# One level of Strassen's scheme in the up projection of a gated MLP, with the down projection cut into four K parts

## The chip, the core and the metric

The kernel runs on one core of a Trainium2 chip. The metric is device time in microseconds for the whole program, from inputs in DRAM to the output in DRAM. The core's engines are named as the profile names them: PE multiplies matrices (PEld is its weight load), DVE, ACT and POOL work element by element, and SP issues transfers. All matrix products accumulate in PSUM; everything else lies in SBUF.

## The reference, cut to what matters

One decoder layer over 528 positions (16 meta tokens and 512 inputs) and 1024 channels. The first half of it (a chunked linear attention branch and a pooling branch, merged by gates) is left out here; the change reaches it only through its buffers. What matters is the second half:

```python
D_FF = 2816
h = h + (gate_a * y_a + gate_b * y_b) @ w_o[l]
hn = rmsnorm(h, norm2_g[l])
up = causal_dwconv(hn @ w_up[l], conv_w[l], conv_b[l])   # three taps
a, bv = jnp.split(up, 2, axis=-1)
h = h + (jax.nn.silu(a) * bv) @ w_down[l]
return rmsnorm(h, final_norm_g)[:, N_META:]
```

`w_up` is 1024 x 5632 and `w_down` is 2816 x 1024, all in float32.

## The kernel before

Activations lie with channels on the 128 partitions and positions along the row, so `h2` is eight tiles of 128 x 528. Each float32 product is made of three products of a shorter format (`F32R`): a tile is split into a high part (an ACT copy that rounds) and a low part (a DVE subtraction of the rounded copy), and hi x hi, hi x lo and lo x hi are accumulated. That is `products` (L112 to L122), with `split` (L217) for activations and `prep_chunk` (L93) for weights.

Weights come in 142 chunks of up to 128 x 1024 in the order of a table (`ORDER`, L46): SP loads a chunk (L91), ACT makes its high part (L102), DVE its low part (L103). Three buffers for the raw chunk and three for the parts let this run ahead of PE by two to three chunks (`chunk`, L105).

The up projection (L582) runs over 22 pairs of 128 output channels, side 0 for `a` and side 1 for `bv`. Each side is one `project`: 8 K tiles x 3 products x 2 halves of the positions (258 and 256 columns), 48 matmuls. DVE multiplies the result by the row's norm factor (L591); ACT and DVE apply the three taps (L594 to L596); ACT applies silu (L598); DVE multiplies the sides (L600), and ACT and DVE split the result into `gh` and `gl` (L601, by L218 and L219). The norm factor itself (`rstd2`) is ready only some microseconds after the first side's matmuls.

The down projection (L618) comes after all 22 pairs: 8 output tiles, each with 66 matmuls over the 22 K tiles, the last one as two halves of 256 positions (L631), behind each of which stands the final norm and the output for that half. A list scheduler of the compiler orders instructions of each engine as their inputs are expected; the engines then run their own lists in order.

SBUF is held by `bigp` (nine buffers of 8 x 528 values per partition) and small pools for weights and work.

Of the kernel before, what the change touches and what calls it, by code (L numbers as in the profile page):

```python
# [15 lines left out]
P = 128  # L16
# [16 lines left out]
UCOLS = (((12, 270), (270, L)), ((10, 270), (270, L)), ((6, 268), (268, L)), FULL)  # L33
SUPERS = [(0, 16)] + [(16 + 128 * i, 128) for i in range(4)]
# [13 lines left out]
for _name, _n in (  # L48
    ("k", 4), ("q", 4), ("v", 8), ("r", 8), ("u", 8), ("ga", 8), ("a", 8),
    ("gb", 8), ("grp", 2), ("b", 8), ("o", 8), ("up", 44), ("down", 24),  # L50
):
    ORDER[_name] = _at
    _at += _n
# [8 lines left out]
def hybrid_block(ctx: ExitStack, tc: tile.TileContext, xt, g1d, wts, wglr, wgk, vecs, out):  # L62
# [10 lines left out]
    def big(name, dt=F32, shape=(KT, L)):  # L73
        return bigp.tile([P, *shape], dt, tag="big", name=name)
# [9 lines left out]
    def load_chunk(j, cuts=None):  # L84
        if j >= NCHUNK or (j in raws and cuts is None):
            return
        nk = 6 if j >= ORDER["down"] and (j - ORDER["down"]) % 3 == 2 else KT
        if j not in raws:
            raws[j] = (wrawp.tile([P, KT, P], F32, tag="wraw", name=f"wraw{j}"), nk)
        for a, b in cuts or ((0, nk),):  # L90
            sp.dma_start(raws[j][0][:, a:b], wts[j, :, a:b])  # L91

    def prep_chunk(j, cuts=None):  # L93
# [3 lines left out]
        t, nk = raws[j]  # L97
# [3 lines left out]
        a, b = cuts or (0, nk)  # L101
# [22 lines left out]
    def project(name, j, xh, xl, cols, hook=None, ahead=PREP_AHEAD):  # L124
        hi, lo = chunk(j, ahead)
        acc = ps(name)
        products(acc, [(hi[:, k], lo[:, k], xh[:, k], xl[:, k]) for k in range(KT)], cols, hook=hook)
# [32 lines left out]
    sp.dma_start(x0[:, 0, 0:264], xt[0, :, 0:264])  # L160
    act.dma_start(g1, g1d)
    load_chunk(0, ((0, 2),))
    sp.dma_start(x0[:, 0, 264:], xt[0, :, 264:])
    load_chunk(1, ((0, 2),))
    sp.dma_start(x0[:, 1], xt[1])
    load_chunk(0, ((2, KT),))
    sp.dma_start(x0[:, 2], xt[2])
    load_chunk(1, ((2, KT),))
    for k in range(3, KT):
        sp.dma_start(x0[:, k], xt[k])  # L170
# [11 lines left out]
    for k in range(KT):  # L182
        for a, b in FULL if k == 0 else ((0, L),):
            act.activation(xh[:, k, a:b], x0[:, k, a:b], AF.Copy, scale=g1[:, k : k + 1])
            dve.scalar_tensor_tensor(xl[:, k, a:b], x0[:, k, a:b], g1[:, k : k + 1], f32(xh[:, k, a:b]), ALU.mult, ALU.subtract)
# [3 lines left out]
        if k >= 2:  # L189
            act.activation(sq1[:, k - 2], x0[:, k - 2], AF.Square)  # L190
# [531 lines left out]
```

## Time and profile before

| what | value |
|---|---|
| three runs | 861.96, 862.66, 862.73 us; median 862.66 |
| the profiled execution | span 860.6 us from its first to its last instruction; its time beside that isn't given, so what lies around it is taken as 862.66 - 860.6 = 2.1 us |
| PE busy | 847.6 us, 98% of the span, granted clock 1.00 between the ends |
| DVE, ACT, POOL busy | 485.0, 345.1, 62.3 us |
| up projection | from 475.9 to 728 us |
| down projection | from 728 to 849.6 us, with 11.0 us behind it |
| moved | 81.13 MB, mean 94 GB/s |

How to read it: a busy share is of the whole span or of a named stretch. A matmul's printed duration (some 282 ns for 258 columns) is longer than the step from one to the next, since matmuls overlap; steps are read from the chain of waits. On DVE, too, the next instruction may start some 0.08 us before the printed end of the one ahead.

### The profile page before, as it was taken

To read this page: it belongs to the slowest core of one execution; us is meant where nothing else is said; L and a number is where in the kernel's file an instruction comes from. 1 tells how busy PE (TensorE), PEld (TensorE's weight loads), DVE (VectorE), ACT (ScalarE), POOL (GpSimd) and SP (SyncE) were. 2 spreads that over 40 slices of the span, in tenths; PEclk is the share of its full clock that TensorE was granted. 3 is DMA by queue.
4 is the path that set the end of the run, shared out by engine and by line. 5 is a ranking of instruction groups with operands and counts; after the bars stand their busy time and mean duration, and the time that the engine had idled before them with its cause. 6 is when DMAs were issued, how large, how long until landed. Compare 5 with 4: busy or idle time off the path is not lost.

```text
span 860.6 us, 15278 instructions
## 1 busy us (share of the span) xinstructions
PE 847.6 (98%) x6627; PEld 824.5 (96%) x6627; DVE 485.0 (56%) x716; ACT 345.1 (40%) x479; POOL 62.3 (7%) x48
## 2 busy tenths in 40 slices
PE   8999999999999999999999999999999999999995
PEld 7999999999999999999999999999999999888884
DVE  6676445389647433355554677667776777332224
ACT  6378243256335212353234544444444444232231
POOL 4000000001740000000012100000000000001011
PEclk9999999999999999999999999999999999999998
DMA  7423311122332333225332333233323332332312
GB/s 241 123 74 99 87 61 50 50 75 74 99 98 75 98 98 99 84 89 196 98 88 85 99 98 85 89 98 99 90 83 98 98 95 79 95 101 85 97 39 98
DMA packets 25939, 81.13 MB, mean 94 GB/s; under 512 B 2864, under 2 KB 5680, under 8 KB 25872
## 3 DMA queue, kind: packets, MB, share of 16 engines
q1 hardware_dynamic: 24384, 78.84, 30.4%
q10 hardware_dynamic: 1488, 1.32, 0.5%
q8 instruction: 52, 0.85, 0.4%
q14 instruction: 15, 0.12, 0.0%
HBM read 78.05 MB, written 2.10 MB: 93 GB/s over the span
## 4 chain that ended last, share of the span: by engine, by line
PE 96%; DVE 1%; ACT 1%; DMA 1%; issue 0%; SPq 0%; DVEq 0%
PE pup L119 29%; PE pv L119 5%; PE pu L119 5%; PE pr L119 5%; PE pga L119 5%; PE po L119 5%; PE pb L119 5%; PE pgb L119 5%; PE pa L119 5%; PE pd L615 5%; PE pd L614 5%; PE pd L616 5%; PE pq L119 3%; PE pk L119 1%; PE pgrp L119 1%; PE po L415 1%
## 5 line engine op out<-in xcount | busy, mean ns | idle before, releaser
L102 ACT ACTIVATE whi<-wraw 128x1024 fp32r<-128x1024 f32 (+2 forms) x146 | 149.2, 1024 | 330.2 <-PE pd L615 71.0
L103 DVE TENSOR_TENSOR wlo<-wraw,whi 128x1024 fp32r<-128x1024 f32 (+2 forms) x146 | 175.9, 1206 | 78.8 <-ACT whi L102 68.8
L119 PE MATMUL pup<-h2l,whi 128*128 128x258 f32 x704 | 141.6, 282 | 0.0
L119 PE MATMUL pup<-h2h,whi 128*128 128x258 f32 x704 | 140.9, 282 | 0.0
L119 PE MATMUL pup<-h2h,wlo 128*128 128x258 f32 x704 | 140.8, 281 | 0.0
L119 PEld LDWEIGHTS pup<-h2h,wlo 128*128 128x128 f32 x704 | 108.8, 188 | 0.0
L119 PEld LDWEIGHTS pup<-h2h,whi 128*128 128x128 f32 x704 | 107.9, 188 | 0.0
L119 PEld LDWEIGHTS pup<-h2l,whi 128*128 128x128 f32 x704 | 107.8, 188 | 0.0
L614 PE MATMUL pd<-gh,whi 128*128 128x512 f32 (+1 forms) x198 | 72.7, 367 | 0.0
L615 PE MATMUL pd<-gl,whi 128*128 128x512 f32 (+1 forms) x198 | 72.4, 365 | 0.0
L616 PE MATMUL pd<-gh,wlo 128*128 128x512 f32 (+1 forms) x198 | 72.3, 365 | 0.0
L591 DVE TENSOR_TENSOR up<-pup,rstd 128x258 f32<-128x258 f32 x88 | 33.5, 421 | 45.9 <-PE pup L119 44.5
L614 PEld LDWEIGHTS pd<-gh,whi 128*128 128x128 f32 x198 | 37.3, 189 | 6.1
L616 PEld LDWEIGHTS pd<-gh,wlo 128*128 128x128 f32 x198 | 37.3, 189 | 6.0
L615 PEld LDWEIGHTS pd<-gl,whi 128*128 128x128 f32 x198 | 37.3, 189 | 6.0
L594 ACT ACTIVATE cv<-up,vec 128x512 f32<-128x512 f32 x44 | 35.9, 816 | 3.8 <-DVE up L591 3.2
L218 ACT ACTIVATE gh<-cv 128x512 fp32r<-128x512 f32 x22 | 13.9, 633 | 55.1 <-DVE cv L600 55.1
L596 DVE SCALAR_TENSOR_TENSOR cv<-up,vec,cv 128x512 f32<-128x512 f32 x44 | 33.1, 752 | 1.5
L595 DVE SCALAR_TENSOR_TENSOR cv<-up,vec,cv 128x512 f32<-128x512 f32 x44 | 32.9, 747 | 1.3 <-ACT cv L594 1.3
L627 POOL TENSOR_TENSOR sq<-sq,n_sq 128x512 f32<-128x512 f32 x6 | 7.8, 1296 | 348.0 <-ACT n_sq L626 348.0
L598 ACT ACTIVATE cv<-cv 128x512 f32<-128x512 f32 x22 | 13.9, 633 | 41.1 <-DVE cv L596 41.1
L574 POOL TENSOR_TENSOR n_sq<-n_sq,n_sq 128x514 f32<-128x514 f32 x7 | 12.4, 1778 | 220.5 <-ACT n_sq L570 220.5
(241 smaller groups left out, 1804.5 us busy)
## 6 DMA issues: line engine op xcount, KB each, us to landing
wraw<-in_wts_dram SPq DMA_DIRECT2D x132, 512.0 KB, 3.6
wraw<-in_wts_dram SPq DMA_DIRECT2D x10, 384.0 KB, 3.1
h<-in_xt_dram SPq DMA_DIRECT2D x1, 2056.0 KB, 8.8
x<-in_xt_dram SPq DMA_DIRECT2D x7, 264.0 KB, 5.9
out_dram<-h ACTq DMA_DIRECT2D x2, 384.0 KB, 2.8
out_dram<-h ACTq DMA_DIRECT2D x2, 256.0 KB, 2.3
out_dram<-h SPq DMA_DIRECT2D x2, 256.0 KB, 2.5
x<-in_xt_dram SPq DMA_DIRECT2D x2, 132.0 KB, 2.4
```

The lines of the kernel that those rows point to most:

```text
L102: act.activation(hi[:, a:b], t[:, a:b], AF.Copy)
L103: dve.tensor_tensor(lo[:, a:b], t[:, a:b], f32(hi[:, a:b]), ALU.subtract)
L119: pe.matmul(acc[:, s, : b - a], w, x[:, a:b], start=(i == 0 and w is wh and x is xh), stop=(i == n - 1 and last),)
L218: act.activation(hi, src, AF.Copy)
L591: dve.tensor_tensor(z[:, c], src, rstd2[:, c], ALU.mult)
L594: act.activation(cv, z[:, META:], AF.Identity, scale=v1("cw2", m), bias=v1("cb", m))
L595: dve.scalar_tensor_tensor(cv, z[:, META - 1 : L - 1], v1("cw1", m), cv, ALU.mult, ALU.add)
L596: dve.scalar_tensor_tensor(cv, z[:, META - 2 : L - 2], v1("cw0", m), cv, ALU.mult, ALU.add)
L598: last = act.activation(cv, cv, AF.Silu)
L614: pe.matmul(acc, hi[:, k], gh[part][:, k, a:b], start=first, stop=False)
L615: pe.matmul(acc, hi[:, k], gl[part][:, k, a:b], start=False, stop=False)
L616: pe.matmul(acc, lo[:, k], gh[part][:, k, a:b], start=False, stop=last)
```

## The change

The up projection's weights are seen as 2 x 2 blocks (two K groups of four tiles each: the even and the odd ones; two sides), and the normalised input as 2 x 2 blocks (two K groups, two halves of the positions, both of 258 columns now; they start at position 12, with zeros in front). One level of Strassen's scheme needs 7 block products for the 8. Each block product is 4 K tiles x 3 = 12 matmuls (`seven`), so a pair takes 84 matmuls where it took 96. The first three pairs (`PLAIN`) still take 96.

The scheme needs sums. On the input side they are made once, after the norm factor is known (`cross`): three blocks as they are (`direct`) and four sums (`crossed`), each split into high and low parts. On the weight side they are made for each pair (`make`): three blocks as they are (`gh`, `gl`) and four sums, in two tiles `sa` and `sb`. On the output side two of the seven products are added by PE in PSUM and the rest by ACT copies and four DVE operations per pair; the norm factor is in the input now and isn't applied again.

The low parts of the three plain weight blocks, and of all down weights, are made another way (`low_by_dma`): POOL writes the negated high part to `gl`, and a transfer issued by POOL adds the float32 weights from DRAM to it. So these weights are read from DRAM twice. `gh` and `gl` have two buffers each.

The down projection is cut into four K parts (6, 6, 6 and 4 tiles). The first three are put between the up pairs, two jobs of two output tiles each behind pairs 8, 9, 14, 15, 19 and 21, and add into `h2`; the last one comes at the end, again with the last tile in two halves, of 12 matmuls now.

The buffers of the first half are made of pairs of tiles in three pools; those that the second half doesn't need are closed before it, and six new pools lie in their place.

```diff
+H0 = 12
+HALF = ((H0, 270), (270, L))
+HN = 258
+PLAIN = 3
+LAG = 2
+PARTS = ((0, 6), (6, 6), (12, 6), (18, 4))
...
-    bigp = ctx.enter_context(tc.tile_pool(name="bigp", bufs=9))
-    wrawp = ctx.enter_context(tc.tile_pool(name="wrawp", bufs=3))
-    whlp = ctx.enter_context(tc.tile_pool(name="whlp", bufs=3))
-    work = ctx.enter_context(tc.tile_pool(name="work", bufs=5))
+    lastp = ctx.enter_context(tc.tile_pool(name="lastp", bufs=12))
+    first = ctx.enter_context(ExitStack())
+    firstp = first.enter_context(tc.tile_pool(name="firstp", bufs=16))
+    midp = first.enter_context(tc.tile_pool(name="midp", bufs=8))
+    wrawp = first.enter_context(tc.tile_pool(name="wrawp", bufs=3))
+    whlp = first.enter_context(tc.tile_pool(name="whlp", bufs=3))
+    work = first.enter_context(tc.tile_pool(name="work", bufs=5))
...
-    s2 = None
+    n2t = wk("n2t")
+    first.close()
+    def phase(name, bufs):
+        return ctx.enter_context(tc.tile_pool(name=name, bufs=bufs, reuse_waits="tile"))
+    rawp, gp, sump, ssp, t3p, unitp = (
+        phase(*a) for a in (("rawp", 2), ("gp", 2), ("sump", 1), ("ssp", 3), ("t3p", 8), ("unitp", 13))
+    )
+    slots = {8: (0, 0), 9: (0, 2), 14: (1, 0), 15: (1, 2), 19: (2, 0), 21: (2, 2)}
+    seq = []
+    for i in range(FF):
+        seq.append(("up", i))
+        if i in slots:
+            part, m = slots[i]
+            seq += [("down", part, m), ("down", part, m + 1)]
+    seq += [("down", 3, m) for m in range(4)]
...
+    def low_by_dma(hi, lo, dram):
+        pool.tensor_scalar(lo, hi, -1.0, 1.0, ALU.mult, ALU.mult)
+        pool.dma_start(lo, dram, accum_op=ALU.add)
...
+    def make(n):
...
+        gh, gl = (gp.tile([P, 3, 512], F32R, tag=f"g{c}", name=f"g{c}{n}") for c in "hl")
+        if job[0] == "down":
+            k = 2 * PARTS[job[1]][1] * P
+            hi, lo = (t.rearrange("p a b -> p (a b)")[:, 0:k] for t in (gh, gl))
+            act.activation(hi, raw.rearrange("p a b -> p (a b)")[:, 0:k], AF.Copy)
+            low_by_dma(hi, lo, wdown[4 * job[1] + job[2], :, 0:k])
...
+            return
+        act.activation(gh, raw[:, 0:3], AF.Copy)
+        low_by_dma(gh, gl, wup[job[1], :, 0:3])
...
+        s = sump.tile([P, 4, 512], F32, tag="sum", name=f"sum{n}")
+        dve.tensor_tensor(s[:, 0::2], raw[:, 3:4].to_broadcast([P, 2, 512]), raw[:, 0:3:2], ALU.add)
+        dve.tensor_tensor(s[:, 1], s[:, 0], raw[:, 2], ALU.add)
+        a = two(f"{n}a")
+        split(*a, parted(s[:, 0:2]))
+        dve.tensor_tensor(s[:, 3], s[:, 1], raw[:, 1], ALU.add)
+        b = two(f"{n}b")
+        split(*b, parted(s[:, 2:4]))
+        ready_w[n] = (g, a, b)
+
+    def weights(n):
+        make(n)
+        make(n + 1)
+        fetch(n + 2)
+        return ready_w[n]
...
+    def cross(i):
...
+        dve.tensor_tensor(t[:, 0:2], b[:, 1:3], b[:, 3:4].to_broadcast([P, 2, HN]), ALU.subtract)
+        dve.scalar_tensor_tensor(t[:, 2], t[:, 0], -1.0, b[:, 2], ALU.mult, ALU.subtract)
+        dve.tensor_tensor(t[:, 3], t[:, 2], b[:, 0], ALU.add)
...
+        split(*d, b[:, 0:3])
...
+        split(*x, t)
...
+    def seven(acc, w, block, x, at, first=True):
+        for k in range(4):
+            for e, (a, b) in enumerate(((0, 0), (0, 1), (1, 0))):
+                pe.matmul(
+                    acc[:, 0:HN], w[a][:, block, k], x[k][b][:, at],
+                    start=first and k == 0 and e == 0, stop=k == 3 and e == 2,
+                    skip_group_check=not first,
+                )
+
+    def up_fast(n, i):
+        g, sa, sb = weights(n)
...
+        seven(x, g, 2, direct, 2)
+        act.activation(z11, x[:, n_], AF.Copy)
+        seven(q, sa, 0, crossed, 1)
+        act.activation(z22, q[:, n_], AF.Copy)
+        seven(v_, g, 0, crossed, 3)
+        seven(x, sa, 1, crossed, 2, False)
+        act.activation(z12, x[:, n_], AF.Copy)
+        seven(y, g, 1, direct, 0)
+        dve.tensor_tensor(z11, y[:, n_], z11, ALU.add)
+        seven(x, sb, 0, crossed, 0, False)
+        act.activation(z21, x[:, n_], AF.Copy, scale=-1.0)
+        dve.tensor_tensor(z22, z21, z22, ALU.subtract)
+        dve.tensor_tensor(z21, v_[:, n_], z21, ALU.add)
+        seven(q, sb, 1, direct, 1, False)
+        dve.tensor_tensor(z12, q[:, n_], z12, ALU.add)
...
+    for n, job in enumerate(seq):
+        if job[0] == "up":
+            i = job[1]
+            (up_plain if i < PLAIN else up_fast)(n, i)
+            if i == 0:
+                for k in range(4):
+                    cross(k)
+            if i >= LAG:
+                conv(i - LAG)
...
+        elif job[1] < 3:
+            w = weights(n)
+            acc = ps(f"pd{n}")
+            for c in range(2):
+                down(acc[:, c], w, c, job[1], (0, 512))
+                h = h2[2 * job[2] + c][:, META:]
+                dve.tensor_tensor(h, acc[:, c], h, ALU.add)
```

How the change moves instructions, at three places. First PE, in the middle of the up projection. Before, one side's matmuls stand in a row (`pup`: a side's PSUM tile; `whi`, `wlo`: its weight chunk):

```order
L119 MATMUL pup_0_5796<-h2l,whi_5662 128x258
L119 MATMUL pup_0_5796<-h2l,whi_5662 128x256
L119 MATMUL pup_0_5796<-h2h,wlo_5663 128x258
L119 MATMUL pup_0_5796<-h2h,wlo_5663 128x256
L119 MATMUL pup_0_5796<-h2h,whi_5662 128x258
L119 MATMUL pup_0_5796<-h2h,whi_5662 128x256
```

Now, at the end of pair 6's fourth product (`xy_6107` is pair 6, `xy_6233` pair 7; `dh`, `dl` are parts of the plain input blocks, `gh_6087` and `gl_6088` the plain weight blocks of pair 7):

```order
L744 MATMUL xy_6107<-xh_5457,sl_6a 128x258
L744 MATMUL xy_6233<-dh_5408,gh_6087 128x258
L744 MATMUL xy_6233<-dl_5409,gh_6087 128x258
L744 MATMUL xy_6233<-dh_5408,gl_6088 128x258 [waits DMASW7_49]
L744 MATMUL xy_6233<-dh_5423,gh_6087 128x258
L744 MATMUL xy_6233<-dl_5424,gh_6087 128x258
L744 MATMUL xy_6233<-dh_5423,gl_6088 128x258
L744 MATMUL xy_6233<-dh_5438,gh_6087 128x258
L744 MATMUL xy_6233<-dl_5439,gh_6087 128x258
L744 MATMUL xy_6233<-dh_5438,gl_6088 128x258
```

The first product of pair 7 stands ahead of the last three of pair 6, and its third matmul waits for the adding transfer (DMASW). The two matmuls that last read the buffers that `gh_6087` and `gl_6088` take over, those of pair 5, are these (`xy_5981`: pair 5):

```order
L744 MATMUL xy_5981<-dh_5438,gl_5836 128x258
L744 MATMUL xy_5981<-dh_5453,gh_5835 128x258
L744 MATMUL xy_5981<-dl_5454,gh_5835 128x258
L744 MATMUL xy_5981<-dh_5453,gl_5836 128x258
L744 MATMUL xy_6107<-dl_5424,gh_5961 128x258
```

Between the fourth of these rows and the matmul that waits stand 70 matmuls.

Second POOL. Before, it has nothing to do between the sums of squares of the second and of the final norm (`n_sq` and `sq`):

```order
L574 TENSOR_TENSOR n_sq_4690<-n_sq_4690,n_sq_5061 128x514 [waits Activation_49,Pool_49]
L574 TENSOR_TENSOR n_sq_4690<-n_sq_4690,n_sq_5123 128x514 [waits Activation_49,Pool_49]
L627 TENSOR_TENSOR sq_7968<-sq_7968,n_sq_8143 128x512 [waits PE_49,Activation_49]
L627 TENSOR_TENSOR sq_7968<-sq_7968,n_sq_8233 128x512 [waits Activation_49,Pool_49]
L627 TENSOR_TENSOR sq_7968<-sq_7968,n_sq_8323 128x512 [waits Activation_49,Pool_49]
```

Now it makes low parts there, 38 times:

```order
L646 TENSOR_SCALAR gl_5962<-gh_5961 128x1536 [waits DMASW4_49,PE_49,Activation_49]
L647 DMA gl_5962<-in_wup_dram 128x1536 [waits Pool_49]
L646 TENSOR_SCALAR gl_6088<-gh_6087 128x1536 [waits DMASW5_49,PE_49,Activation_49]
L647 DMA gl_6088<-in_wup_dram 128x1536 [waits Pool_49]
L646 TENSOR_SCALAR gl_6214<-gh_6213 128x1536 [waits DMASW6_49,PE_49,Activation_49]
```

Each negation waits for PE to have left the buffer and for ACT's high part, and each transfer for the negation.

Third DVE. Before, this is one pair's work (`up`: a side times the norm factor; `cv`: the taps):

```order
L591 TENSOR_TENSOR up_0_6741<-pup_0_6692,rstd_5130 128x258
L591 TENSOR_TENSOR up_0_6741<-pup_0_6692,rstd_5130 128x256
L103 TENSOR_TENSOR wlo_6750<-wraw_6562,whi_6749 128x1024
L595 SCALAR_TENSOR_TENSOR cv_0_6744<-up_0_6741,vec,cv_0_6744 128x512
L596 SCALAR_TENSOR_TENSOR cv_0_6744<-up_0_6741,vec,cv_0_6744 128x512
L591 TENSOR_TENSOR up_1_6804<-pup_1_6755,rstd_5130 128x258
L591 TENSOR_TENSOR up_1_6804<-pup_1_6755,rstd_5130 128x256
L103 TENSOR_TENSOR wlo_6815<-wraw_6625,whi_6814 128x1024
L595 SCALAR_TENSOR_TENSOR cv_1_6807<-up_1_6804,vec,cv_1_6807 128x512
L596 SCALAR_TENSOR_TENSOR cv_1_6807<-up_1_6804,vec,cv_1_6807 128x512
L600 TENSOR_TENSOR cv_1_6807<-cv_0_6744,cv_1_6807 128x512
L219 TENSOR_TENSOR gl_5135<-cv_1_6807,gh_5132 128x512
```

Now a stretch of the same length, with work of three pairs in it (`sum`: weight sums, `sl`: their low parts, `z`: the output sums):

```order
L766 TENSOR_TENSOR z_6106<-xy_6107,z_6106 128x258
L789 TENSOR_TENSOR cv_6201<-cv_6201 128x512
L678 TENSOR_TENSOR sum_6218<-raw_6104 128x2x512
L785 SCALAR_TENSOR_TENSOR cv_6327<-z_5980,vec,cv_6327 128x512
L769 TENSOR_TENSOR z_6106<-z_6106 128x258
L248 TENSOR_TENSOR g_6210<-cv_6201,g_6210 128x512
L770 TENSOR_TENSOR z_6106<-zv_6108,z_6106 128x258
L679 TENSOR_TENSOR sum_6218<-sum_6218,raw_6104 128x512
L786 SCALAR_TENSOR_TENSOR cv_6327<-z_5980,vec,cv_6327 128x512
L682 TENSOR_TENSOR sum_6218<-sum_6218,raw_6104 128x512
L772 TENSOR_TENSOR z_6106<-zv_6108,z_6106 128x258
L785 SCALAR_TENSOR_TENSOR cv_6327<-z_5980,vec,cv_6327 128x512
```

A pair's 12 operations have become 15, over more elements, and they are mixed with those of the pairs beside it.

More of the change, by code (lines that the diff above doesn't have):

```diff
@@ L627, in hybrid_block @@
             pool.tensor_tensor(tot3, tot3, sq, ALU.add)
-        act.activation(h3[:, m], h3[:, m], AF.Copy, scale=v1("gf", m))
-    parts = [chunk(ORDER["down"] + 21 + part) for part in range(3)]
+        act.activation(h, h, AF.Copy, scale=v1("gf", m))
+    w = weights(base + 3)
     accs = []
@@ L632, in hybrid_block @@
         acc = ps(f"pd7_{a}")
-        down(acc[:, 0, 0:256], parts, (a, b))
+        down(acc[:, 0, 0:256], w, 1, 3, (a, b))
         if a:
```

395 lines of the change are left out of this document (248 added, 147 removed).

## The prediction

> **What bounds the kernel now.** I read the page's totals first, then its chain, then the busy time by stage.
>
> ```profile
> span 860.6 us, 15278 instructions
> PE 847.6 (98%) x6627; PEld 824.5 (96%) x6627; DVE 485.0 (56%) x716; ACT 345.1 (40%) x479; POOL 62.3 (7%) x48
> ...
> PE 96%; DVE 1%; ACT 1%; DMA 1%; issue 0%; SPq 0%; DVEq 0%
> ```
>
> PE is busy for 98% of the span, and the chain that ended last is PE for 96%. So only fewer PE steps shorten this kernel, and any wait put on PE lengthens it. From the chain comes the length of a step, and the rows by stage (columns: length, then busy time of PE, PEld, DVE, ACT, POOL with counts, granted clock, DMA share, GB/s) say how much room the other engines have in the stages that change:
>
> ```profile
> 482.10 245.97 PE pup L119 x2064
> ...
> 482.10:728.00 245.90, 245.90 (x2066) 245.90 (x2065) 177.05 (x261) 110.54 (x135) 0.00 (x0) 1.00 0.31 92
> 728.00:849.60 121.60, 121.60 (x600) 103.38 (x599) 38.11 (x43) 33.84 (x41) 9.31 (x7) 1.00 0.27 81
> 849.60:860.60 11.00, 1.17 (x5) 0.37 (x3) 5.01 (x8) 1.31 (x3) 1.50 (x1) 0.68 0.37 126
> ```
>
> Up projection: PE never idle, DVE 177 of 246 us (72%), ACT 45%, POOL empty. A step is 245.97 / 2064 = 0.119 us. Down: PE never idle either, DVE at a third.
>
> **PE's own work.** Up had 22 x 96 = 2112 matmuls and has 3 x 96 + 19 x 84 = 1884. The clock stays at 1.00, so 228 x 0.119 = **-27.2 us**. The columns (258 for 258 and 256) change nothing worth a term. Down keeps its arithmetic; its 512-column step follows from the stores into `h`:
>
> ```profile
> L621 DVE TENSOR_TENSOR h<-pd,h x7: 691/692/692, 743.1 to 832.9; 128x512 f32<-128x512 f32 x7
> ```
>
> Six tiles of 66 in 89.8 us: 0.227 us each. There are 54 more of these (12.2 us) and 108 fewer with 256 columns (12.9 us): **-0.6 us**.
>
> **The tail.** The last output tile's second half covers the norm of its first half. Of the chain:
>
> ```profile
> 849.66 0.02 issue
> 849.68 0.43 DVE h L641
> ```
>
> PE ends at 849.6 and the span 11.0 us later. The cover was 66 half-wide matmuls, 7.9 us; it is 12, 1.4 us. So the first half's three output multiplies on DVE (0.69 each by the L600 row below) can now fall among the second half's: at most about 4 us with the transfer behind them, at least 0. I take **+2 us**.
>
> **DVE.** A fast pair has three weight sums, one over 1024 values and two over 512; two low parts of 1024; four output sums of 258; four taps; the product and its low part. Their nearest rows (columns: count, then busy us, mean ns):
>
> ```profile
> L103 DVE TENSOR_TENSOR wlo<-wraw,whi 128x1024 fp32r<-128x1024 f32 x132 | 165.3, 1253 | 73.6 <-ACT whi L102 63.6
> L596 DVE SCALAR_TENSOR_TENSOR cv<-up,vec,cv 128x512 f32<-128x512 f32 x44 | 33.1, 752 | 1.5
> L591 DVE TENSOR_TENSOR up<-pup,rstd 128x258 f32<-128x258 f32 x44 | 18.8, 426 | 45.9 <-PE pup L119 44.5
> L600 DVE TENSOR_TENSOR cv<-cv,cv 128x512 f32<-128x512 f32 x22 | 15.2, 692 | 0.7
> ...
> 603.12 1.23 DVE L103 TENSOR_TENSOR wlo<-wraw,whi 128x1024 fp32r<-128x1024 f32 x1
> 604.27 0.75 DVE L595 SCALAR_TENSOR_TENSOR cv<-up,vec,cv 128x512 f32<-128x512 f32 x1
> ...
> L591 DVE TENSOR_TENSOR up<-pup,rstd x88: 413/420/427, 486.2 to 728.5; 128x258 f32<-128x258 f32 x44, 128x256 f32<-128x256 f32 x44
> ```
>
> 3 x 1.25 + 2 x 0.69 + 4 x 0.43 + 4 x 0.75 + 2 x 0.69 = 11.2 us. The next instruction starts before the printed end of the one ahead (603.12 + 1.23 against 604.27), 0.08 us each time, so 15 of them take 10.0 us. PE takes 84 x 0.119 = 10.0 us for a pair. That is parity: DVE goes from 72% of this stage to nearly all of it in runs of fast pairs, and recovers in the down jobs, where the four stores of 0.69 of a slot meet some 16 us of PE.
>
> `cross` adds some 21 us of DVE work once, and nobody can start on it before the norm factor (486.2). From there to the low parts of pair 8, DVE's order holds 117 operations, 76 us start to start, so 562.2; PE reaches pair 8 at 475.9 + 3 x 11.4 + 5 x 10.0 = 560. That is 2 us late, up to 11 if POOL blocks DVE (below). But PE will by then have lost 10 us to the wait of the next part, which covers it: **0**, bounds 0 and 11.
>
> ACT keeps room: per pair the plain high parts (1.49, below), two of 1024 at 1.06, four output copies, two taps and two of 512:
>
> ```profile
> L594 ACT ACTIVATE cv<-up,vec 128x512 f32<-128x512 f32 x44 | 35.9, 816 | 3.8 <-DVE up L591 3.2
> L218 ACT ACTIVATE gh<-cv 128x512 fp32r<-128x512 f32 x22 | 13.9, 633 | 55.1 <-DVE cv L600 55.1
> L542 ACT ACTIVATE pbh<-pgrp,vec 128x258 fp32r<-128x258 f32 x8 | 3.8, 472 | 0.3 <-PE pgrp L119 0.2
> ```
>
> 1.49 + 2.12 + 1.89 + 1.63 + 1.27 = 8.4 of 10.0 us. Nil, with that 1.6 us as its cover. The relaid pools, `h2` loaded in four pieces, and the copies in the first half go with it: all lie ahead of waits of PE that DMA or ACT had met long before, and PE has no idle time there now.
>
> **The added wait.** The plain low parts are the only new thing that can stop PE. `gh` and `gl` have two buffers, so a job's chain cannot begin before PE has read the last of the job two earlier: ACT's high part, POOL's negation, the adding transfer, then PE. Call its length C. PE is in order, so everything behind the third matmul of the new product waits with it, and POOL, also in order, holds the next negation and transfer behind one that waits.
>
> ```profile
> GB/s 241 123 74 99 87 61 50 50 75 74 99 98 75 98 98 99 84 89 196 98 88 85 99 98 85 89 98 99 90 83 98 98 95 79 95 101 85 97 39 98
> DMA  7423311122332333225332333233323332332312
> wraw<-in_wts_dram SPq DMA_DIRECT2D x132, 512.0 KB, 3.6
> wraw<-in_wts_dram SPq DMA_DIRECT2D x10, 384.0 KB, 3.1
> L102 ACT ACTIVATE whi<-wraw 128x1024 fp32r<-128x1024 f32 x132 | 139.8, 1060 | 306.8 <-PE pd L615 49.9 <-PE pup L119 38.7 <-PE pa L119 36.6
> L102 ACT ACTIVATE whi<-wraw 128x768 fp32r<-128x768 f32 x8 | 6.8, 847 | 21.1 <-PE pd L615 21.1
> L258 POOL MEMSET early_r<- 128x1024 int32 x1 | 1.0, 957 | 0.0
> L248 POOL MEMSET early<- 128x528 f32 x1 | 0.5, 538 | 0.0
> L500 POOL TENSOR_TENSOR pt<-u 128x1054 f32<-128x1054 f32 x1 | 1.9, 1946 | 0.2 <-DVE u L233 0.2
> L574 POOL TENSOR_TENSOR n_sq<-n_sq,n_sq 128x514 f32<-128x514 f32 x7 | 12.4, 1778 | 220.5 <-ACT n_sq L570 220.5
> L627 POOL TENSOR_TENSOR sq<-sq,n_sq 128x512 f32<-128x512 f32 x6 | 7.8, 1296 | 348.0 <-ACT n_sq L626 348.0
> ```
>
> - High part, 1536 values: 213 ns per 256 values, so 1.06 + 2 x 0.21 = 1.49 us.
> - Negation: no row has it. Memsets grow by 0.84 ns a value, so 1.4 us; two inputs cost 1.85 ns a value, so 2.8 us. It has one input and is nearest to the memset; with a little for the read, 1.5. POOL beside a busy DVE took 1.78 us where it took 1.30 beside an idle one (L574, L627), so 0.4 more; bounds 0 and 0.4.
> - Transfer, 768 KB: no adding transfer is in the trace. A plain one, by 0.5 us for each 128 KB over 512 KB, takes 4.6 us; at the first slice's 241 GB/s in 7 tenths (344 GB/s) it moves in 2.3 us over a fixed 1.6, so 3.9. If reading the destination doubles the part that grows with size, these are 7.6 and 6.2. Bounds 3.9 and 7.6; I take the middle of the four, 5.6.
> - Four hand-overs at some 0.05 us, as the 0.02 of the chain's row: 0.2.
>
> C is 1.49 + 1.5 + 0.4 + 5.6 + 0.2 = **9.2 us**, bounds 7.0 and 12.5.
>
> The page "Collectives: The Full Stack" of the Trainium skill, section "The bandwidth ceiling: the fold count and why AG ≠ RS ≠ AR", says that an addition in the transfer halves its rate because it reads two sources. With "DMA: Bandwidth & Descriptors", section "Anatomy of one DMA — SWDGE (gpsimd) path" (2.0 us plus size over 436 GB/s), this transfer would take an estimated 3.8 us as a plain one and 5.6 us with two reads, so C would be 7.4 or 9.2. No run here shows either yet.
>
> Against C stands the work that PE has between the last read of a buffer pair and the first read of the next `gl` in it, counted in its order: 44 matmuls for pair 4, then 56, 67, 70, 63 (5.2, 6.7, 8.0, 8.4, 7.5 us); 7.6 to 7.2 for pairs 11 to 14 and 17 to 19 and for 21; 6.8 to 7.7 for the first down job of a slot, 10.6 to 11 for the second; 8.8 to 9.0 for the up job behind two downs; 5.6 to 6.0 for three of the last four jobs, whose 512 KB make C 6.9 (1.06 + 1.0 + 0.4 + 4.2 + 0.2). The shortfalls at 9.2: pairs 4 to 8 10.2; six first downs 11.7; five pairs behind downs 1.9; eight other pairs 14.0; the last part 3.1: 41 us. A wait of one job lengthens some leads of the next; walked job by job, with each wait pushing what follows, 35 remain: **+35 us**. The same walk gives 4 us at C 7.2, 13.5 at 8.0, 25 at 8.7, 60 at 10.4, 73 at 11, 108 at 12.5.
>
> **Sum.** 860.6 - 27.2 - 0.6 + 2 + 0 + 35 = 869.8 us of span. The median of the runs is 862.66, 2.1 above this span, which I keep: **872 us**. Without the wait it would be 837; 862.66 is reached with 26 us of wait, at C 8.7, a transfer of 5.1 us.
>
> **Rivals.** *Quick transfer, faster.* If the transfer lands in 4.4 us or less, C is at most 8.0 and the wait at most 13.5: 850 or less, 840 at the lower bound. For it: DMA is busy for a third of the time in this stage, and there are sixteen engines to spread over. Against: it comes behind SP's 1 MB loads, and traffic goes from 92 GB/s to (1.05 + 0.79 MB) / 10.0 us = 184. It decides below C 8.7. By the fit of the Trainium skill's page "DMA: Bandwidth & Descriptors" (the section named above) for a plain transfer alone it would be an estimated 3.8 us, on this side.
>
> *Slow transfer or negation, much slower.* With a doubled slope and load, or POOL at its two-input rate, C is 10.5 to 12.5: 11 gives 910, 12.5 gives 945. For it: POOL and DVE do disturb each other when both read SBUF:
>
> ```profile
> 214.08 6.38 POOL L500 TENSOR_TENSOR pt<-u 128x1032 f32<-128x1032 f32 x1 [10.06 <-DVE u L233]
> ...
> 219.29 2.25 DVE L103 TENSOR_TENSOR wlo<-wraw,whi 128x1024 fp32r<-128x1024 f32 x1
> ...
> 221.47 2.39 DVE L479 TENSOR_TENSOR o<-o,r 128x514 f32<-128x514 f32 x1
> ```
>
> POOL took 6.4 us where the 1054-wide one took 1.9, and DVE took 2.25 and 2.39 where it takes 1.25 and 0.69. Against: the negation has one input only.
>
> *DVE becomes the bound.* The transfer is quick, but each of some 34 negations holds DVE up by most of its 1.5 us, so parity is lost: 11 us at the first fast pairs, 7.5 over pairs 10 to 14, 6 over 16 to 19, 25 together: 862, no change. Against: down jobs give DVE time to catch up.
>
> **Chances.** Forecast (C 8.7 to 10.4, 862 to 896) 0.36; quick transfer 0.35; slow 0.19; DVE 0.10, even on both sides. A difference of 0.2% is about what a measurement of this kernel tells from none. Faster: 0.35 + 0.01 (the forecast's lower edge) + 0.04 = 0.40; same 0.03 + 0.02 = 0.05; slower 0.32 + 0.19 + 0.04 = 0.55. The range, 842 (C 7.5, no tail cost) to 912 (C 11.1), leaves out the ends of both C's, 2 in 10; the forecast's own is 862 to 896.
>
> **What would show it.** PE's step stays 0.119 and its busy time falls by 28 us. The list of PE's waits shows 35 us, nearly all ended by the adding transfer, first at pair 4 (4 us), then at most jobs (0.5 to 2 us). The negation reads 1.5 to 2 us, the transfer 5.6 from issue to landing. Should PE's waits end on DVE (`sl` or the output sums) instead, the third rival holds; should they stay under 14 us, the first. A step of PE that has changed, or waits in the first half, would make the whole sum wrong.

## The result, and the profile after

The changed kernel takes 945.56 us (median; 945.09 to 949.28) against 862.32 us of the kernel before on the same chip: a ratio of 1.0975, 95% interval 1.0955 to 1.0994. It is slower by 83 us: outside the range of 842 to 912, though on the side that was forecast.

The page's totals after the change:

```profile
span 943.7 us, 14947 instructions
PE 855.7 (91%) x6345; PEld 812.1 (86%) x6345; DVE 547.8 (58%) x801; ACT 396.4 (42%) x589; POOL 152.2 (16%) x129
```

PE has 282 matmuls fewer (228 in the up projection; in the down projection 108 half-wide ones became 54 whole ones), and yet is busy for 8 us more, in a span in which it idles for 88 us. The two kernels from 470 us to the end (columns as in the prediction; before, then after):

```profile
470.00:860.60 390.60, 380.77 (x2768) 361.75 (x2766) 226.16 (x321) 151.41 (x185) 14.34 (x10) 0.99 0.30 90
```

```profile
470.00:943.70 473.70, 389.33 (x2476) 350.03 (x2474) 287.68 (x402) 199.04 (x279) 99.81 (x82) 0.94 0.53 131
```

The whole difference lies here, 473.7 against 390.6, and the granted clock fell from 0.99 to 0.94. What PE waited for (what ended the wait, us in total, times, the longest):

```profile
PE xy L744 <- DMA gl<-in_wup_dram: 30.9, 16, 5.0
PE pd L799 <- DMA gl<-in_wdown_dram: 15.1, 6, 3.2
PE xy L744 <- DVE z L717: 11.1, 1, 11.1
PE pe L799 <- DMA gl<-in_wdown_dram: 5.4, 3, 2.6
PE zv L744 <- DVE z L770: 4.9, 8, 0.9
PE zv L744 <- ACT z L761: 2.8, 3, 1.0
```

The adding transfer ends 51.4 us of waits. One wait of 11.1 us is for DVE to empty PSUM at the first fast pair, and 7.7 us are for the output copies and sums of the pair ahead. The rows of transfers (KB each, us from issue to landing) and of POOL's negation (busy, mean ns):

```profile
gl<-in_wup_dram POOLq DMA_DIRECT2D x22, 768.0 KB, 7.4
gl<-in_wdown_dram POOLq DMA_DIRECT2D x12, 768.0 KB, 7.1
gl<-in_wdown_dram POOLq DMA_DIRECT2D x4, 512.0 KB, 5.8
...
L646 POOL TENSOR_SCALAR gl<-gh 128x1536 fp32r<-128x1536 f32 x34 | 52.8, 1552 | 384.5 <-ACT gh L665 273.6 <-ACT gh L661 111.0
```

One chain in full, from the order of time, for the second down job of a slot (start, length, engine; in brackets the idle time and what ended it):

```profile
621.36 0.39 PE L799 MATMUL pd<-g,gl 128*128 128x512 f32 x1
621.60 1.48 ACT L661 ACTIVATE gh<-raw 128x1536 fp32r<-128x1536 f32 x1 [7.39 <-PE pd L799]
623.18 1.46 POOL L646 TENSOR_SCALAR gl<-gh 128x1536 fp32r<-128x1536 f32 x1 [6.22 <-ACT gh L661]
624.95 0.89 POOL L647 DMA_DIRECT2D gl<-in_wdown_dram  x1 [0.30 <-POOL gl L646]
632.44 0.50 PE L799 MATMUL pd<-g,gl 128*128 128x512 f32 x1 [1.93 <-DMA gl<-in_wdown_dram]
```

PE leaves the buffer at 621.6, and the new low part is there at 632.44: C is 10.8 us, where 9.2 was forecast. The chain is not an odd one: over the 28 jobs (pairs and down jobs) between the first six and the last four, the median from the start of ACT's high part to the landing is 10.7 us. Two landed much later, after 10.1 and 9.6 us in place of 5.7 to 8.4: they are the two that were issued within 0.3 us of a raw load, and behind them stand the two longest of these waits on PE, 5.0 and 4.5 us.

The last piece is a step of PE that is not constant any more. Three stretches, the first of which holds a wait of 3.1 us that ends at 598.1:

```profile
594.70:598.10 3.40, 0.38 (x2) 0.00 (x0) 2.34 (x4) 0.60 (x2) 0.00 (x0) 1.00 0.49 98
598.10:602.40 4.30, 4.26 (x19) 3.90 (x20) 1.02 (x2) 1.45 (x2) 0.00 (x0) 0.63 0.01 4
602.40:606.00 3.60, 3.60 (x22) 3.19 (x22) 2.58 (x3) 2.33 (x4) 2.35 (x2) 0.97 0.61 217
...
602.16 0.42 PE L744 MATMUL xy<-xh,sh_8b 128*128 128x258 f32 x1
602.38 0.40 PE L744 MATMUL xy<-xl,sh_8b 128*128 128x258 f32 x1
602.59 0.30 PE L744 MATMUL xy<-xh,sl_8b 128*128 128x258 f32 x1
602.73 0.28 PE L744 MATMUL xy<-xh,sh_8b 128*128 128x258 f32 x1
602.85 0.28 PE L744 MATMUL xy<-xl,sh_8b 128*128 128x258 f32 x1
```

Behind the wait the granted clock is 0.63 for 4.3 us and a matmul follows the one ahead by 0.22 us, then by 0.12 again. The trace's records of the clock show ten such stretches before the tail, at half the clock, 3.4 to 10.2 us long and 48 us together, each behind a wait of 1.8 us or more. Seven other waits of 1.9 to 3.2 us have none. Counted over the starts of PE's matmuls, 147 steps with 256 or 258 columns took 0.20 to 0.22 us: 147 x (0.215 - 0.119) = 14 us. The Trainium skill's page "TensorE: Matmul & The Clock Gate", section "HAM oscillation — how this bites in real kernels", has waits for data between short stretches of matmuls send PE back to half its clock each time. This trace agrees on the slow rate, with 0.215 against 0.119, and not on each time: ten of 17 such waits.

What tells the ten from the seven can be read from the same records. All ten stretches begin a whole number of times 3.413 us after the first of them, so the clock here changes on a fixed grid. In this trace, an interval of that grid in which PE idled for 1.81 us or more (just over half of it) was followed by one at half the clock each time, and one in which it idled for 1.74 us or less never was. The wait of 3.2 us at 829.7 has no slow stretch behind it: two intervals share it, 1.6 us each. Over this trace and those of the runs below, from the up projection to the tail, all 59 full-rate intervals with 1.81 us or more of idle time had a slow one behind them, and of those with less only one had (1.66 us, run nine).

### The profile page after: what moved, and what is told of

It reads as the page before. It is cut to its first block, busy times and chain, and to the rows that moved or that the text cites. A ratio compares the mean times of both kernels' runs of the same rounds, so it can differ in the third digit from the quotient of the medians.

```text
span 943.7 us, 14947 instructions
## 1 busy us (share of the span) xinstructions
PE 855.7 (91%) x6345; PEld 812.1 (86%) x6345; DVE 547.8 (58%) x801; ACT 396.4 (42%) x589; POOL 152.2 (16%) x129
## 5 line engine op out<-in xcount | busy, mean ns | idle before, releaser
L131 ACT ACTIVATE whi<-wraw 128x1024 fp32r<-128x1024 f32 (+2 forms) x78 | 79.0, 1015 | 206.9 <-PE pa L148 36.4
L646 POOL TENSOR_SCALAR gl<-gh 128x1536 fp32r<-128x1536 f32 (+1 forms) x38 | 56.9, 1498 | 402.8 <-ACT gh L665 273.6
L132 DVE TENSOR_TENSOR wlo<-wraw,whi 128x1024 fp32r<-128x1024 f32 (+2 forms) x78 | 94.8, 1217 | 13.2 <-ACT whi L131 7.2
L799 PE MATMUL pd<-g,gh 128*128 128x512 f32 (+1 forms) x304 | 96.6, 397 | 1.4 <-DVE h L823 1.4
L744 PE MATMUL xy<-dh,gl 128*128 128x258 f32 x152 | 49.3, 327 | 30.9 <-DMA gl<-in_wup_dram 30.9
L799 PE MATMUL pd<-g,gl 128*128 128x512 f32 (+1 forms) x152 | 59.9, 400 | 15.1 <-DMA gl<-in_wdown_dram 15.1
L799 PEld LDWEIGHTS pd<-g,gh 128*128 128x128 f32 x304 | 56.6, 194 | 13.1 <-DVE h L823 2.6
L744 PE MATMUL xy<-dh,gh 128*128 128x258 f32 x152 | 47.7, 316 | 11.2 <-DVE z L717 11.1
L785 DVE SCALAR_TENSOR_TENSOR cv<-z,vec,cv 128x512 f32<-128x512 f32 x44 | 33.6, 775 | 35.6 <-ACT cv L784 35.6
L744 PE MATMUL xy<-dl,gh 128*128 128x258 f32 x152 | 47.4, 313 | 0.0
L786 DVE SCALAR_TENSOR_TENSOR cv<-z,vec,cv 128x512 f32<-128x512 f32 x44 | 38.7, 886 | 0.7
```

Of the source, the lines that this page charges most:

```text
L131: act.activation(hi[:, a:b], t[:, a:b], AF.Copy)
L132: dve.tensor_tensor(lo[:, a:b], t[:, a:b], f32(hi[:, a:b]), ALU.subtract)
L646: pool.tensor_scalar(lo, hi, -1.0, 1.0, ALU.mult, ALU.mult)
L744: pe.matmul(acc[:, 0:HN], w[a][:, block, k], x[k][b][:, at], start=first and k == 0 and e == 0, stop=k == 3 and e == 2, skip_group_check=n ...
L785: dve.scalar_tensor_tensor(cv, z[:, c, META - 1 : L - 1], v1("cw1", m), cv, ALU.mult, ALU.add)
L786: dve.scalar_tensor_tensor(cv, z[:, c, META - 2 : L - 2], v1("cw0", m), cv, ALU.mult, ALU.add)
```

## Experiments

**One: the same transfer without the addition.**

```diff
-        pool.dma_start(lo, dram, accum_op=ALU.add)
+        pool.dma_start(lo, dram)
```

> The changed kernel with plain transfers in place of the adding ones: the negation stands, the transfer then overwrites it, so the low parts of these weights are left out (raw weights lie in their place). Theory A (the destination's read makes the transfer slow): from issue to landing 4.6 to 5.0 us in place of 7.1 to 7.4, the chain from PE's last read to the new low part 8.3 us in place of 10.9, PE's waits on these transfers fall from some 58 to some 15 us, the time to 885 to 895 us. Theory B (any transfer from POOL's queue is this slow): landing stays at 7 us and the time within 10 us of 945.

This kernel leaves out the low parts of these weights: raw weights lie in their place. Measured: 899.1 us, ratio 1.0426 (1.0405 to 1.0447).

```profile
gl<-in_wup_dram POOLq DMA_DIRECT2D x22, 768.0 KB, 5.4
gl<-in_wdown_dram POOLq DMA_DIRECT2D x12, 768.0 KB, 5.8
raw<-in_wdown_dram SPq DMA_DIRECT2D x12, 768.0 KB, 4.3
...
PE pd L799 <- DMA gl<-in_wdown_dram: 7.6, 4, 2.6
PE xy L744 <- DMA gl<-in_wup_dram: 6.3, 8, 2.4
PE pe L799 <- DMA gl<-in_wdown_dram: 2.4, 2, 1.3
```

The addition costs 1.3 to 2.0 us of a transfer, and POOL's queue another 1.1 to 1.5 against SP's for the same 768 KB. Theory A holds in kind and is off in size (5.4 to 5.8 us, not 4.6 to 5.0). With C shorter by less than 2 us, PE's waits on the transfers fall from 51.4 to 16.3 us, the steps at half speed from 147 to 50, and the time by 46 us. C is now 1.5 + 1.5 + 0.3 + 5.6 + 0.3 = 9.2 us, the very value of the forecast; and the time is 899, not 872. So of the 73.6 us by which the changed kernel missed the forecast, 46.5 hang on the addition in the transfer, and 27.1 would have been missed with C as forecast.

**Two and three: no transfer; POOL, or DVE, subtracts.** The raw tile is handed over in place of the address in DRAM.

```diff
-        pool.tensor_scalar(lo, hi, -1.0, 1.0, ALU.mult, ALU.mult)
-        pool.dma_start(lo, dram, accum_op=ALU.add)
+        pool.tensor_tensor(lo, raw, f32(hi), ALU.subtract)   # three: dve
```

> The changed kernel with the plain low parts made by one POOL subtraction of raw and high part, no transfer. Theory A (the length of the chain with the transfer sets PE's waits, and the slow PE steps follow from the waits): the chain is 1.5 + 2.9 + 0.1 = 4.5 us, under every lead, so these waits vanish and most of the 22 us of slow steps with them; what stays is the 11 us at the first fast pair and some 15 us of waits for PSUM: 860 to 872 us. Theory C (POOL and DVE hold each other up, and DVE has no room): 38 subtractions of 2.9 us or more hold DVE up by 2 us and more each, DVE becomes the bound: 890 us or more.

Measured: 966.6 us, ratio 1.1213 (1.1195 to 1.1232).

```profile
PE 860.1 (89%) x6345; PEld 819.8 (85%) x6345; DVE 610.5 (63%) x801; ACT 395.1 (41%) x589; POOL 195.2 (20%) x91
...
PE zv L743 <- DVE z L769: 37.1, 14, 3.0
...
L646 POOL TENSOR_TENSOR gl<-raw,gh 128x1536 fp32r<-128x1536 f32 x34 | 124.1, 3649 | 378.9 <-ACT gh L664 275.6 <-ACT gh L660 103.2
```

Theory C: the same DVE instructions, the same count of 801, take 610.5 us where they took 547.8, a POOL subtraction takes 3.65 us where 2.8 was the price of a two-input row, and PE now waits for DVE (for POOL's low parts themselves only 7.8 us, in five waits). The Trainium skill's page "SBUF — State Buffer", section "Who interferes with whom", has a DVE instruction with two SBUF inputs and a GpSimd instruction that reads SBUF exclude each other; this run agrees, with the 610.5 us.

> The changed kernel with the plain low parts made by DVE, no transfer and no POOL work. Each pair costs DVE 1.8 us more, 11.8 us against PE's 10.0. Theory A: no wait on a transfer, but DVE is the bound in runs of fast pairs, 19 x 1.8 = 34 us less what the down jobs give back, so 880 to 900 us, with PE's waits ended by DVE. Theory C' (DVE had more room than counted): 870 us or less.

Measured: 867.0 us, ratio 1.0054 (1.0034 to 1.0075).

```profile
PE 834.7 (96%) x6345; PEld 797.8 (92%) x6345; DVE 586.8 (68%) x839; ACT 395.1 (46%) x589; POOL 62.8 (7%) x53
...
PE xy L743 <- DVE z L716: 11.7, 1, 11.7
...
545.00:565.00 20.00, 19.27 (x149) 18.02 (x148) 19.17 (x28) 11.46 (x19) 0.00 (x0) 1.00 0.16 53
```

The time lies in the range of theory C' (870 us or less), though DVE had no more room than counted: it is the bound in stretches, as theory A has it, but the down jobs give the time back. DVE took 38 operations more, and the kernel is 78 us faster than the changed one: the waits on transfers, those for output sums and the POOL work all go at once, and steps at half speed fall to 23. DVE is the bound for these stretches only (between 545 and 565 us it is busy for 19.2 of 20, and PE does 149 matmuls where 168 would fit). The one long wait, 11.7 us, stays.

**Four: three pieces of 256 KB.** Each of the three plain blocks has its own high and low tile, negation and adding transfer.

```diff
+        for e in (2, 0, 1):
+            act.activation(gs[e][0], raw[:, e], AF.Copy)
+            low_by_dma(*gs[e], wup[job[1], :, e])
```

> The changed kernel with the plain blocks in three pieces of 256 KB, each with its own high and low tile, negation and adding transfer. A piece's buffer is free once its 12 matmuls are done, and its chain is 0.6 + 0.5 + 0.3 + some 4.7 + 0.3 = 6.4 us against leads of 8.6 us and more. Theory A: the waits on these transfers vanish, and most of the slow steps with them; the 11 us at the first fast pair and some 15 us of waits for PSUM stay: 860 to 875 us. Theory D (the transfers are slow because they share the DMA engines with the raw loads, or POOL's queue is full): the pieces land no sooner than 7 us, waits stay above 30 us, 900 us or more.

Measured: 911.8 us, ratio 1.0578 (1.0535 to 1.0620).

```profile
gl<-in_wup_dram POOLq DMA_DIRECT2D x66, 256.0 KB, 5.1
raw<-in_wup_dram SPq DMA_DIRECT2D x22, 1024.0 KB, 6.9
...
PE xy L757 <- DMA gl<-in_wup_dram: 18.5, 7, 4.4
```

Neither theory holds whole: the waits fell from 51.4 to 18.5 us, under the 30 of theory D, but did not vanish as in theory A; the time is in theory D's range (900 us or more). A third of the bytes still took 5.1 us, and the raw loads beside them went from 5.1 to 6.9, so it seems that the transfers disturb each other; which of the two delays ended the seven waits was not told apart.

**Five and six: the order of the input sums; four plain pairs.** Both with DVE's subtractions.

```diff
-            if i == 0:
-                for k in range(4):
+            if i < 2:                       # six: PLAIN = 4, and if i < 4: cross(i)
+                for k in (2 * i, 2 * i + 1):
                     cross(k)
```

> The run with DVE's subtractions (867.0 us), and besides it the input sums (cross) made two behind pair 0 and two behind pair 1 in place of four behind pair 0. There PE waited 11.7 us at the first fast pair for DVE to empty PSUM, since DVE's order held all of cross ahead of that. Theory F (the order alone makes this wait): pair 1's products leave PSUM before the second half of cross, 8 to 11 us of it go, 856 to 859 us. Theory G (DVE has that much work there in any order): the wait moves to the low parts of the first fast pair, 864 us or more.

Measured: 868.0 us, ratio 1.0064 (1.0049 to 1.0079).

```profile
PE zv L743 <- ACT xh L247: 2.8, 2, 1.6
PE zv L743 <- DVE xl L248: 2.5, 2, 1.8
```

The long wait went, as in theory F, but six waits of 0.6 to 1.8 us, 7.3 us together, for the parts of the input sums took its place (four of them in these rows), as in theory G, and the time did not change. DVE has that work there in this order too.

> The run with DVE's subtractions, with four plain pairs in place of three and one input sum behind each of them. PE does 12 matmuls more, 1.4 us. Theory F: the whole wait of 11.7 us goes, 855 to 858 us, and DVE, which was the bound in runs of fast pairs, has one pair less of it. Theory G: 864 us or more.

Measured: 859.8 us, ratio 0.9972 (0.9962 to 0.9983). Between the two ranges, nearer to F: with one more plain pair on PE and the input sums spread over four pairs, most of the wait is gone; some 10 us are still lost between 510 and 590 us.

**Seven: ACT negates in place of POOL.** The changed kernel, transfer and all.

```diff
-        pool.tensor_scalar(lo, hi, -1.0, 1.0, ALU.mult, ALU.mult)
+        act.activation(lo, raw, AF.Copy, scale=-1.0)
```

> The changed kernel (945.6 us) with the negated high part written by ACT from the raw weights in place of POOL's negation; the adding transfer stands. The chain keeps its length, 1.5 + 1.5 + 0.3 + 7.3 + 0.3 us. Theory H (POOL's negation holds DVE up, some 0.7 us each time, and the 13 us of waits for PSUM come from that): DVE's busy time falls from 548 to some 525 us, the waits ended by DVE's output sums go, the waits on the transfers stay: 925 to 935 us. Rival: ACT, then at 9.9 of 10.0 us for each pair, delays the chain and the output copies: 945 us or more.

Measured: 978.0 us, ratio 1.1340 (1.1286 to 1.1393).

```profile
PE 876.9 (89%) x6345; PEld 833.1 (85%) x6345; DVE 528.1 (54%) x801; ACT 444.7 (45%) x627; POOL 94.7 (10%) x91
...
gl<-in_wup_dram POOLq DMA_DIRECT2D x22, 768.0 KB, 8.9
gl<-in_wdown_dram POOLq DMA_DIRECT2D x12, 768.0 KB, 9.4
...
PE xy L744 <- DMA gl<-in_wup_dram: 46.1, 14, 5.2
PE pd L799 <- DMA gl<-in_wdown_dram: 20.5, 7, 5.4
```

The half of theory H on DVE holds: without POOL's negations its busy time falls from 547.8 to 528.1, 0.5 us for each, and the waits for output sums from 4.9 to 1.0. The time went the other way, into the rival's range (945 us or more) but not by its path: ACT's links of the chain are as long as POOL's were, and transfers now land after 8.9 to 9.4 us. A raw buffer is given back when its last reader is done, which is now ACT's negation, so the load that refills it and the adding transfer are issued together (at 611.6 and 611.9 us at one slot), where they mostly were 1.8 us apart. That this overlap is what lengthens them was not isolated by a run, but the other traces bear it out: in the changed kernel the two adding transfers issued within 0.3 us of a raw load took 10.1 and 9.6 us and all others 5.7 to 8.4; in run eleven nine such took 9.0 to 10.9 and all others 5.4 to 8.7.

**Eight: no Strassen.** DVE's subtractions, all 22 pairs plain and so no input sums, the K parts as they are. The part of the edit that is not shown puts the gated tiles into the memory that is left free.

```diff
-PLAIN = 3
+PLAIN = 22
...
```

> The run with DVE's subtractions with all 22 pairs plain (no sums, 96 matmuls each) and the K parts of the down projection where they are; the freed memory holds the gated tiles. PE's matmuls alone give 836 + 27 = 863 us. Theory I (what that run lost over 836 us, some 31 us, comes from the sums: the wait behind cross and DVE as the bound): it goes with them, 862 to 868 us, so that the scheme's gain was eaten by its own sums. Rival: the loss comes from the down parts between the pairs or slower steps, and stays: 880 us or more.

Measured: 866.1 us, ratio 1.0042 (1.0027 to 1.0057).

```profile
PE 848.1 (98%) x6573; PEld 818.4 (95%) x6573; DVE 493.9 (57%) x735; ACT 337.4 (39%) x486; POOL 62.9 (7%) x53
```

Theory I: from the up projection on PE waits nowhere but in the tail. With DVE's subtractions, everything in the change but the scheme costs 3.6 us, of which the longer tail is 3. Run three, with the scheme and 27 us less of PE's work, takes 867: what came with the scheme ate its whole gain. That is mostly the wait behind the input sums (11.7) and, counted from the starts of matmuls, some 11 us of pauses too short to be listed, of which run eight has 2.4.

**Nine, ten, twelve: fewer fast pairs, shorter runs of them.** From run six: down jobs one at a time (nine), six plain pairs (ten), both (twelve); the loop that reads `slots` changes with it.

```diff
-PLAIN = 4
+PLAIN = 6
-    slots = {8: (0, 0), 9: (0, 2), 14: (1, 0), 15: (1, 2), 19: (2, 0), 21: (2, 2)}
+    slots = {7: (0, 0, 1), 8: (0, 1, 1), 9: (0, 2, 2), 13: (1, 0, 1), 14: (1, 1, 1), 15: (1, 2, 2), 19: (2, 0, 1), 20: (2, 1, 1), 21: (2, 2, 2)}
...
```

> The run with four plain pairs and DVE's subtractions (859.8 us), with the down jobs spread more evenly: one behind pairs 7, 8, 13, 14, 19 and 20, two behind 9, 15 and 21, in place of two behind each of six pairs. Theory I (DVE is the bound in runs of fast pairs, 11.8 against 10.0 us, and catches up in down jobs): the longest run falls from 5 pairs to 4, the loss of some 1 us per 20 us and the one of 11 us between 510 and 590 shrink: 853 to 858 us. Rival: the first part's gated tiles are not ready behind pair 7, and PE waits for them: 860 us or more.

Measured: 858.8 us, ratio 0.9954 (0.9937 to 0.9970): less than theory I had it, and no wait for the first part either; not told apart from run six by the intervals alone. Its trace has a slow stretch of 6.8 us behind a wait of 1.5 us at 524.6 (22 steps, some 2.5 us); run six's trace has the same wait and no slow stretch.

> The same run with six plain pairs in place of four. PE does 24 matmuls more, 2.9 us. Theory I: most of what is lost between 510 and 590 us (10 us) is DVE catching up with the input sums; two more plain pairs give it 2 x 2.9 us: 855 to 860 us. Rival (the loss is per fast pair and each still gains): 862 to 863 us.

Measured: 855.4 us, ratio 0.9920 (0.9905 to 0.9935). Theory I: 2.9 us more of PE's work, and 4.4 us less time.

> Both of the last changes together: six plain pairs and the down jobs spread singly, with DVE's subtractions. If DVE is still what is lost in runs of fast pairs (some 0.8 us in each 20 us between 590 and 830), the shorter runs give some of that back, as they gave 1.0 us with four plain pairs: 853 to 855 us. If what is left in each 20 us has another cause (the longer steps of the down matmuls, waits on ACT's copies), no change: 855 to 856 us.

Measured: 853.7 us, ratio 0.9903 (0.9886 to 0.9919), faster than both kernels of this case, by 1% against the one before; in the range of the first theory, that DVE is still what is lost.

```profile
span 851.9 us, 14897 instructions
PE 833.5 (98%) x6381; PEld 798.5 (94%) x6381; DVE 574.0 (67%) x827; ACT 388.6 (46%) x574; POOL 62.8 (7%) x53
```

Of the 22.9 us that 16 fast pairs save on PE (16 x 12 x 0.119), 12.4 arrive against run eight, or 10.7 in run ten, whose down jobs stand as in run eight.

**Eleven: PE's idle time filled.** The changed kernel, with matmuls whose result nobody reads ahead of each fast pair's wait.

```diff
+        for e in range(20):
+            pe.matmul(x[:, 300:512], g[0][:, 2, e % 4], direct[e % 4][0][:, 2][:, 0:212], start=True, stop=True)
         seven(x, g, 2, direct, 2)
```

> The changed kernel (945.6 us) with 20 further matmuls of 212 columns for each fast pair, ahead of the matmul that waits for the adding transfer, into columns of PSUM that nobody reads; the computation is as before. They add 19 x 20 x 0.1 = 38 us of PE work, nearly all of it in time in which PE would wait. Theory J (PE's idle time itself halves the granted clock for some microseconds behind it, and the 147 steps of 0.215 us come from that): the waits at the fast pairs fall from some 30 to under 12 us, the half-speed steps to under 70, and the time stays within 12 us of 945. Theory K (the slow steps come from the transfers' load on memory, or from elsewhere): the waits fall, but the half-speed steps stay at 120 or more, and the time rises to 955 or more.

Measured: 983.9 us, ratio 1.1409 (1.1386 to 1.1432).

```profile
PE zv L744 <- DVE z L772: 14.7, 13, 1.1
PE xy L744 <- ACT z L766: 12.0, 14, 0.9
...
PE xy L744 <- DVE z L768: 8.4, 13, 0.8
```

The steps at half speed fell from 147 to 46 (16 of them added matmuls), and the stretches at half the clock from ten to four, with as many transfers as before: theory J in that. The time is outside J's range; it fits K's (955 us or more), but by K the slow steps would have stayed at 120 or more, and the slow stretch shown above had the DMA engines busy for 0.01 of it, with 4 GB/s. The added matmuls did not stay in one place: between 690 and 704 us, for instance, they run in four groups. Behind three of them stand short waits for PSUM, 2.6 us of idle time in such a pair by the rows above, which took the place of the one for the transfer: none fills half of an interval of the clock's grid, and together they cost more. So the run shows that the slow steps go with the long waits, and not what the kernel would take without them.

## Why the prediction was wrong

Two steps of the prediction failed. The added wait was worked out with a transfer of 5.6 us in C, which took 7.1 to 7.4; and a wait was taken to cost PE its own length and no more, with DVE's lateness put at 0 and PE's step at 0.119 us throughout. The span is 73.9 us above the sum's 869.8. Counted by pieces, 16.4 of that are in the term for the added wait (51.4 measured for 35), and 57.5 in terms that were 0, missing or too small. By run one the addition alone is worth 46.5 us of time: 35 in the waits that the transfers end (51.4 to 16.3), some 9 in slow steps (147 to 50).

**PE's work** was right in its count, 282 matmuls fewer. The step is 0.121 us in place of 0.119 and the wide one 0.232 in place of 0.227 (medians over the trace), so the down term of -0.6 us was about +2, and the whole of PE's work some 5 us more than counted. **The tail** was right: 13.9 us for 11.0, so +2.9 for +2.

**The DVE term of 0 failed.** The working looked for the first late operation at the low parts of pair 8 and let the transfers' waits cover it. What came late was nearer: DVE's order has all four input sums ahead of the products of pairs 1 and 2, PE had no PSUM left, and stood for 11.1 us at pair 3, before any wait on a transfer. The bound of 11 was there; the cover was not. Another order alone does not help (run five). The term's count of DVE's work per pair, 10.0 us, held: with 1.8 us more in run three it was the bound for stretches only.

**The transfer in C was too short:** 5.6 us forecast, 7.1 to 7.4 measured. The high part (1.49) and the negation (1.5, without the 0.4 for the port in the median) were right; the hand-over to the transfer took 0.3. C is 10.8, inside its bounds and inside the second rival (C from 10.5), which had a chance of 0.19. The prediction took the middle of four values; the nearest is the highest, 7.6, with a doubled slope on the plain transfer's 4.6. That it was near is luck: the addition costs 1.3 to 2.0 us, which is not a doubling (beyond the prediction's fixed 1.6 us, 3.8 became 5.8 and 4.2 became 5.5), and the plain transfer through POOL's queue is already at 5.4 to 5.8. The estimate by the Trainium skill's pages in the prediction had 1.8 us for the second read, 3.8 to 5.6, and the runs agree with that difference; what it had too low is the plain transfer, 3.8 for 5.4 to 5.8. The Trainium skill's page "Collectives: The Full Stack", section "The bandwidth ceiling: the fold count and why AG ≠ RS ≠ AR", states the halving for a reduction in a ring of cores, which no run here has.

**The walk over the jobs was too high, and what it left out too large.** At C 10.9 it gives 71 us and so 908; measured are 51.4. At 9.2, run one, it gives 35; measured are 16.3. That other waits fall into the leads and lengthen them would explain it, and was not counted. On the other side stand losses that had no term. From 834.8 us (860.6 - 27.2 - 0.6 + 2) to 943.7:

| piece | us |
|---|---|
| waits ended by the adding transfers | 51.4 |
| first fast pair, for DVE | 11.1 |
| other waits for PSUM (4.9, 2.8, 1.4 and 0.3) | 9.4 |
| steps at half speed | 14 |
| longer steps, the tail | 6 |
| rest | 17 |

The rest is what is left over. Counted from the starts of matmuls, what could make it up comes to 21 us, a little more than the rounded rows leave: 98 pauses too short to be listed 12, the steps at 41 waits beyond their idle time 7, wide steps at half speed 2.

The claim that PE's step stays 0.119 us was the one that hid the fourth row: a wait on PE was priced at its own length, while it also slows what follows. And POOL was priced as an engine that costs nobody anything: its 38 negations held DVE up by 0.5 us each (run seven), which shows in the third row: without them its 4.9 us became 1.0.

**The rivals.** The second came true in its first half, the slow transfer (the negation was not slow), and its price at this C, some 908, was short by 38 us. The first (quick transfer) would have given 850; even without any transfer (run three) the time is 867, so that the 837 us "without the wait" were out of reach by 30: the wait at the first fast pair, 11.7, and some 17 of short pauses, longer steps and slow steps. The third (DVE becomes the bound) had the hold-up by the negations in it, at most of 1.5 us each; 0.5 was measured, and beyond the first fast pair DVE was not the bound.

## What to carry to other kernels

A chain through three engines and a transfer, with two buffers, must be shorter than the work between the last read of one user and the first read of the next but one; price each link from a row, and where the trace has no row for a link, run that link before building on it. A long wait on PE costs more than its length: here, where 1.81 us or more of it fell into one interval of 3.413 us, the matmuls ran at the slow step, 0.215 us for 0.119, for the next 3.4 us, so that a wait of 3.2 us could be free of this and one of 1.8 not. A scheme that saves PE's work by sums elsewhere pays only as far as the engine that makes the sums has room within the runs of that work. Here fewer fast pairs (16 for 19) and the plainest place for the low parts, DVE, made 853.7 us of 945.6.

## What the runs showed of the hardware that was not expected

- One POOL instruction with a single input holds DVE up, too: 38 of 1.5 us added 19.7 us to DVE's busy time; 38 subtractions with two inputs added 82 (610.5 against 528.1).
- A transfer of 768 KB took 4.3 us from SP's queue, 5.4 to 5.8 from POOL's, 7.1 to 7.4 with the addition; 256 KB with it took 4.8 to 5.1, so that cutting it shortens it little. Issued within 0.3 us of a raw load, the adding one of 768 KB took 9.6 and 10.1 us.
- PE's clock was halved for whole intervals of a grid of 3.413 us (stretches of 3.4, 6.8 and 10.2 us; the one of 10.2 began within the wait of 11.1 and ended 3.7 us behind it). Each stretch began behind an interval with 1.81 us or more of idle time, but for one behind 1.66.
